# The head of a two-layer decoder trunk on one core: where its small loads are issued, how x is scaled, and in what order its first steps stand

## The chip, the core and the metric

The kernel runs on one core of one Trainium2 chip. The metric is device time in microseconds (us); the figure for a kernel is the median of its runs. Engines: TensorE (PE, its weight loads PEld), VectorE (DVE), ScalarE (ACT), GpSimd (POOL), and SyncE (SP), which issues most DMAs. The engines work side by side, each through its own list of instructions in a fixed order; they wait for one another on semaphores.

## What is computed

A hybrid decoder trunk over 256 tokens of width 1024: two layers, each of three parts (a half-step SwiGLU FFN, a mixer, another FFN). Every part begins with an RMS norm and a shift and a scale that come from a conditioning vector c. Only the start matters here:

```python
cond = jax.nn.silu(c)
mod = (cond @ ada_w[i] + ada_b[i]).reshape(B, N_SUB, 3, 1, D)
h = rms_norm(x, norm_g[i, 0]) * (1.0 + mod[:, 0, 1]) + mod[:, 0, 0]
x = x + 0.5 * mod[:, 0, 2] * swiglu(h, ffn_w_up[i, 0], ffn_w_down[i, 0])
```

Before any product of the first FFN can be made, two slices of `ada_w` (scale and shift) have to be loaded and multiplied by `cond`. All is float32; the kernel gets there by splitting each operand into a high part (float32r) and a low part, and by three matmuls for each product (high x high, high x low, low x high).

## The kernel before, in words

**The head.** The first FFN starts with seven of its 22 column blocks at once (`HEAD = 7`: three accumulators in the pool `mm`, four in the pool `aux`), and goes through the contraction in eight steps of 128 (q = 0 to 7). What a step needs, and the words used for it below:

- *chain q*: the 1 MB piece of `ada_w` for this step (two buffers), multiplied by `cond` on VectorE in eight instructions (lines 430 and 432, tile `adc`).
- *sums q*: eight small matmuls on TensorE that add the chain up over the partitions (line 444, tile `adac`), and then three tiny VectorE instructions (lines 450 and 453, tile `headmod`), which give shift and scale.
- *casts and low splits q*: the 0.9 MB weight piece (two buffers, a and b) is cast on ScalarE to its high part (line 356, `wh`), and VectorE subtracts it for the low part (line 357, `wl`).
- *shift q*: ScalarE makes `u` from the normed x (line 583) and its high part (line 586); VectorE makes the low part (line 587, *low h q*).
- *products q*: 42 matmuls (lines 726 to 728), seven blocks x two halves x three.

**The order.** Each load, cast, chain and so on is written into the program in a certain order, and a list scheduler then fixes each engine's order when the kernel is built: at each point it takes, of the instructions that it holds to be ready, the one written first. `issue_after(i)` adds that an instruction stands behind i on i's engine. In the loop of lines 577 to 592, step q writes chain q+1, then sums q and shift q, then products q-1; while products are written, each group of three calls `tick`, which writes one more piece of the next splits (`pump`, up to two weight pieces ahead). The VectorE part of sums q is put behind `last_chain`, the chain that was written last: chain q+1. So chain 1 stands ahead of sums 0.

**The loads.** All large loads go through SP's queue into eight buffers of 512 KB (`raw`), in the order in which they are used: chain 0, weights 0, chain 1, weights 1, and so on; a buffer is loaded again when its last reader is done. The two halves of x come before them. Six small loads (norm gains, `ada_b`, three more vectors, constants; lines 515 to 520) are issued in between, two behind each of the first three large ones (lines 524 to 528).

**The rest of the start.** ScalarE squares x; POOL makes the reciprocal root (line 556); TensorE transposes x and ScalarE copies it to `self.x` (line 614); VectorE scales x by the root (line 559, two instructions of 128x1024) and TensorE and ScalarE do the same for the scaled x (`xn`). Two groups of transposes (lines 561 and 566) turn the small rows into columns `vec` and `adab`, which the sums need.

**After the head** the other 15 blocks follow with 48 matmuls each, then the down projection, and then the five other parts; the products of these are spread with loads and splits in the same manner.

## Time and profile before

| | |
|---|---|
| median of 3 runs | 1098.29 us (1098.12 to 1099.98) |
| profiled execution | 1097.96 us, its span 1096.2 us |
| PE / DVE / ACT busy | 98% / 81% / 54% of the span |
| DMA | 260.26 MB, mean 237 GB/s, about 330 GB/s up to 150 us |
| first product of the head starts | 21.20 us |

How the rows are read: in a timeline a row is start (us), duration (us), engine, line, operation, output<-inputs, shapes, count, and in brackets the idle time of the engine before it with what ended it; several instructions of one kind in a row are one line. SPq and the like are the engine's sequencer, which issues DMAs. A window row gives, for a stretch of time, the busy time of each engine with its number of instructions, then TensorE's granted clock, the busy share of the DMA engines and GB/s.

### The profile page before, as it was taken

Reading aid. Unit: us, or ns where it says so; the run is one execution under the profiler, and the core shown is the slowest. Engines: PE = TensorE matmul, PEld = TensorE weight load, DVE = VectorE, ACT = ScalarE, POOL = GpSimd, SP = SyncE. Lnnn points to the kernel's source line nnn. Section 1 sums busy time; section 2 is a strip of 40 time slices with the busy share of each in tenths; the row PEclk is TensorE's granted clock in tenths of the full one; section 3 lists DMA queues with packets and bytes.
Section 4 is the critical chain, followed back from the end, with each engine's and each line's share of the span. In section 5 each row is a group of like instructions: output and inputs, shape, how many; then the busy total and the mean of one; then the engine's idle time right before and its main releaser. Section 6 shows DMA issues by size and latency. Waiting matters only on the chain.

```text
span 1096.2 us, 22151 instructions
## 1 busy us (share of the span) xinstructions
PE 1072.4 (98%) x8835; PEld 1049.2 (96%) x8835; DVE 883.3 (81%) x1598; ACT 586.7 (54%) x1105; POOL 23.1 (2%) x46
## 2 busy tenths in 40 slices
PE   6999999999999999999999999999999999999997
PEld 6999999988899999999999999999998999999997
DVE  6989999589895999888779999977987879555542
ACT  5364444486864754433555444445677756444443
POOL 0000000010000000000000000000000000000000
PEclk9999999999999999999999999999999999999999
DMA  9999999569774589999959999985653356665530
GB/s 299 335 332 331 329 322 320 169 211 352 243 248 117 154 272 329 298 285 303 263 173 274 320 329 350 313 241 173 192 154 116 117 164 191 185 190 176 177 113 39
DMA packets 304707, 260.26 MB, mean 237 GB/s; under 512 B 9524, under 2 KB 281500, under 8 KB 304604
## 3 DMA queue, kind: packets, MB, share of 16 engines
q1 hardware_dynamic: 304172, 257.80, 77.0%
q8 instruction: 69, 1.13, 0.4%
q0 software_dynamic: 288, 0.52, 0.2%
q10 hardware_dynamic: 144, 0.52, 0.1%
q14 instruction: 34, 0.28, 0.1%
HBM read 257.77 MB, written 1.05 MB: 236 GB/s over the span
## 4 chain that ended last, share of the span: by engine, by line
PE 62%; issue 19%; DVE 9%; DMA 5%; ACT 3%; POOL 1%; SPq 0%; POOLq 0%; DVEq 0%; ACTq 0%
PE pf L727 13%; PE pf L726 13%; PE pf L728 13%; PE pd L726 5%; PE pd L728 5%; PE pd L727 5%; DMA raw<-in_ada_w_dram 5%; DVE wl L368 3%; DVE adaacc L408 2%; ACT wh L367 1%; PE pA L1170 1%; PE pv L879 1%; PE pv L877 1%; PE pv L878 1%; PE sc L996 1%
## 5 line engine op out<-in xcount | busy, mean ns | idle before, releaser
L727 PE MATMUL pf<-hbuf,wh 128*128 128x256 f32 (+1 forms) x1920 | 542.0, 283 | 0.9 <-DVE hbuf L587 0.9
L728 PE MATMUL pf<-hbuf,wl 128*128 128x256 f32 (+1 forms) x1920 | 540.7, 283 | 0.0
L726 PE MATMUL pf<-hbuf,wh 128*128 128x256 f32 (+1 forms) x1920 | 537.8, 284 | 0.6 <-ACT hbuf L586 0.6
L367 ACT CAST wh<-raw 128x1024 fp32r<-128x1024 f32 x338 | 341.3, 1026 | 289.8 <-PE pf L727 158.3
L368 DVE TENSOR_TENSOR wl<-raw,wh 128x1024 fp32r<-128x1024 f32 x338 | 400.5, 1193 | 110.3 <-ACT wh L367 109.4
L727 PEld LDWEIGHTS pf<-hbuf,wh 128*128 128x128 f32 x1920 | 362.8, 189 | 2.2 <-DVE hbuf L587 1.6
L726 PEld LDWEIGHTS pf<-hbuf,wh 128*128 128x128 f32 x1920 | 361.8, 190 | 1.0 <-ACT hbuf L586 0.6
L728 PEld LDWEIGHTS pf<-hbuf,wl 128*128 128x128 f32 x1920 | 362.4, 189 | 0.2 <-issue 0.2
L728 PE MATMUL pd<-gx,wl 128*128 128x256 f32 x704 | 196.5, 279 | 1.1 <-DVE wl L368 1.1
L726 PE MATMUL pd<-gx,wh 128*128 128x256 f32 x704 | 197.2, 280 | 0.0
L727 PE MATMUL pd<-gx,wh 128*128 128x256 f32 x704 | 196.3, 279 | 0.0
L408 DVE SCALAR_TENSOR_TENSOR adaacc<-raw,cond,adaacc 128x1024 f32<-128x1024 f32 x112 | 143.4, 1280 | 17.5 <-DMA raw<-in_ada_w_dram 16.5
L728 PEld LDWEIGHTS pd<-gx,wl 128*128 128x128 f32 x704 | 132.6, 188 | 1.5 <-DVE wl L368 1.5
L726 PEld LDWEIGHTS pd<-gx,wh 128*128 128x128 f32 x704 | 133.4, 189 | 0.1
L727 PEld LDWEIGHTS pd<-gx,wh 128*128 128x128 f32 x704 | 132.3, 188 | 0.0
L792 ACT CAST gx<-g 128x256 fp32r<-128x256 f32 x88 | 35.6, 407 | 78.2 <-DVE g L834 70.9
L794 DVE TENSOR_TENSOR gx<-g,gx 128x256 fp32r<-128x256 f32 x88 | 36.7, 419 | 0.2
L834 DVE TENSOR_TENSOR g<-sa,pf 128x256 f32<-128x256 f32 x73 | 30.1, 414 | 0.3 <-ACT sa L833 0.2
L799 DVE SCALAR_TENSOR_TENSOR x<-pd,mod,x 128x256 f32<-128x256 f32 x32 | 14.3, 479 | 19.5 <-PE pd L728 19.5
L460 DVE STREAM_TRANSPOSE adatr<-adaacc 128x256 f32<-128x256 f32 x64 | 28.3, 442 | 1.4
L461 DVE TENSOR_REDUCE adared<-adatr 128x8 f32<-128x256 f32 x64 | 26.7, 418 | 1.6
L833 ACT ACTIVATE sa<-pf 128x256 f32<-128x256 f32 x73 | 27.4, 376 | 0.0
(219 smaller groups left out, 872.8 us busy)
## 6 DMA issues: line engine op xcount, KB each, us to landing
raw<-in_ffn_w_up_dram SPq DMA_DIRECT2D x162, 512.0 KB, 5.9
raw<-in_ada_w_dram SPq DMA_DIRECT2D x128, 512.0 KB, 6.0
raw<-in_ffn_w_down_dram SPq DMA_DIRECT2D x76, 512.0 KB, 5.5
raw<-in_fox_w_in_dram SPq DMA_DIRECT2D x32, 512.0 KB, 5.2
raw<-in_hgrn_w_in_dram SPq DMA_DIRECT2D x32, 512.0 KB, 4.1
raw<-in_ada_w_dram SPq DMA_DIRECT2D x32, 256.0 KB, 6.6
raw<-in_ffn_w_up_dram SPq DMA_DIRECT2D x16, 448.0 KB, 6.0
raw<-in_fox_w_out_dram SPq DMA_DIRECT2D x8, 512.0 KB, 4.6
```

Source lines behind the costliest of these rows:

```text
L367: nc.scalar.copy(wh[:, ks, cs], raw)
L368: nc.vector.tensor_tensor(wl[:, ks, cs], raw, wh[:, ks, cs].bitcast(F32), ALU.subtract)
L408: nc.vector.scalar_tensor_tensor(self.ada_acc, raw, self.cond[:, k:k + 1], self.ada_acc, ALU.mult, ALU.add)
L460: nc.vector.transpose(tr, total[:, o:o + S])
L461: nc.vector.tensor_reduce(red[:, o // 32:(o + S) // 32], tr.rearrange("p (b j) -> p b j", j=32), AX.X, ALU.add)
L726: nc.tensor.matmul(ps, wh, hx[:, :n], start=first, stop=False, skip_group_check=True)
L727: nc.tensor.matmul(ps, wh, hx[:, lo:lo + n], start=False, stop=False, skip_group_check=True)
L728: nc.tensor.matmul(ps, wl, hx[:, :n], start=False, stop=last, skip_group_check=True)
L792: nc.scalar.copy(dst[:, :S], v)
L794: nc.vector.tensor_tensor(dst[:, lo:lo + S], v, dst[:, :S].bitcast(F32), ALU.subtract)
L833: nc.scalar.activation(sa, ps[0], AF.Silu)
L834: nc.vector.tensor_tensor(g, sa, ps[1], ALU.mult)
```

## The change

It touches the head alone:

- The six small loads go to GpSimd's queue, ahead of the large loads in the program; SP issues only c, the identity, x and the large ones.
- x is copied to `self.x` by ScalarE and VectorE in turn (two copies each). x is scaled by ScalarE instead of VectorE, in pairs of 128 columns with their transposes and copy right behind each pair: eight instructions of 128x256 for two of 128x1024.
- The transposes for `vec` and `adab` share one PSUM bank.
- Shift 0 comes ahead of the loop. Sums 0 no longer stand behind chain 1, but behind the first low split of weights 0 (`first_low`). The casts of weights 1 stand behind the high part of h 0, and chain 1 behind low h 0.
- Products q are written in two pieces, blocks 0 to 2 (`HEAD_CUT = 3`) and blocks 3 to 6, and sums and shift q+1 stand between them. Written ahead of sums q+1 by the ticks of the first piece are, for q = 0, chain 1 and splits 1 (its second piece writes chain 2 and splits 2), and for q >= 1 chain q+2 and splits q+2: so `last_chain` of sums 2 is still chain 3, of sums 3 chain 4, and so on; sums 1 now stand behind chain 1.

```diff
@@ -1,5 +1,5 @@
 import math
-from contextlib import ExitStack
+from contextlib import ExitStack, nullcontext
 
 import numpy as np
 
@@ -38,7 +38,7 @@
 HEAD = 7
 QW = 128
 NPE = 0
-DEEP = 3
+HEAD_CUT = 3
 HG_LAG = (4, 3, 4, 10, 12)
 FOX_LAG = (24, 6)
 HG_ORDER = [("hgq", 0), ("hgv", 0), ("hgq", 1), ("hgq", 2), ("hgv", 1), ("hgq", 3),
@@ -353,8 +353,11 @@
                 for cs in cuts:
                     raw = self.take_raw()
                     raw = raw if HEAD > 4 else raw[:, 0, :]
-                    nc.scalar.copy(wh[:, k, cs], raw)
-                    nc.vector.tensor_tensor(wl[:, k, cs], raw, wh[:, k, cs].bitcast(F32), ALU.subtract)
+                    with self.tc.issue_after(self.last_shift[0]) if p[1] == 1 else nullcontext():
+                        nc.scalar.copy(wh[:, k, cs], raw)
+                    v = nc.vector.tensor_tensor(wl[:, k, cs], raw, wh[:, k, cs].bitcast(F32), ALU.subtract)
+                    if p[1] == 0 and cs.start == 0:
+                        self.first_low = v.ins
                     yield
             self.ready[i] = (kind, wh, wl)
             return
@@ -427,7 +430,8 @@
                                          start=first, stop=False, skip_group_check=True)
                         first = False
                 elif k < NPE + 2:
-                    nc.vector.tensor_scalar(ac[:, k % 2], raw[:, i, :], self.cond[:, k:k + 1], None, ALU.mult)
+                    with self.tc.issue_after(self.last_shift[1]) if q == 1 else nullcontext():
+                        nc.vector.tensor_scalar(ac[:, k % 2], raw[:, i, :], self.cond[:, k:k + 1], None, ALU.mult)
                 else:
                     v = nc.vector.scalar_tensor_tensor(ac[:, k % 2], raw[:, i, :], self.cond[:, k:k + 1],
                                                        ac[:, k % 2], ALU.mult, ALU.add)
@@ -446,7 +450,7 @@
         for part in (1, 0):
             b = l * 72 + (s * 3 + part) * 8 + q * n
             m = self.head_mod[:, part, q * n:(q + 1) * n]
-            with self.tc.issue_after(self.last_chain):
+            with self.tc.issue_after(self.last_chain if q else self.first_low):
                 nc.vector.tensor_tensor(m, ps[:, part * n:(part + 1) * n], self.adab[:, b:b + n], ALU.add)
             if part == 1:
                 g = (l * 3 + s) * 8 + q * n
@@ -520,12 +524,10 @@
                  (cst, a["consts"][:, P:])]
         for dst, src in small[:2]:
             nc.sync.dma_start(dst, src)
-        small = small[2:]
+        for dst, src in small[2:]:
+            nc.gpsimd.dma_start(dst, src)
         while len(self.raw_queue) < RAW_BUFS:
             self.emit_raw()
-            for dst, src in small[:2]:
-                nc.sync.dma_start(dst, src)
-            small = small[2:]
         self.ones = cp.tile([P, P], F32, name="ones")
         nc.vector.memset(self.ones, 1.0)
         self.selq = cst[:, 128:144]
@@ -554,28 +556,30 @@
             nc.scalar.activation(xs[t], xt[t], AF.Square, accum_out=ms[:, t:t + 1])
         nc.vector.tensor_scalar(ms, ms, 1.0 / D, EPS, ALU.mult, ALU.add)
         self.last_pow = nc.gpsimd.tensor_tensor(ms, ms, self.mhalf, ALU.pow).ins
-        self.load_x(xt, self.x)
-        for t in range(2):
-            nc.vector.tensor_scalar(xs[t], xt[t], ms[:, t:t + 1], None, ALU.mult)
+        self.load_x(xt, self.x, engines=(nc.scalar.copy, nc.vector.tensor_copy))
+        self.vec = cp.tile([P, 80], F32, name="vec")
+        self.adab = cp.tile([P, 144], F32, name="adab")
+        self.head_mod = cp.tile([P, 2, KC], F32, name="headmod")
         pr = self.bank("pr")
-        nc.tensor.transpose(pr[:, :80], rows, self.ident[:80, :80])
-        self.vec = cp.tile([P, 80], F32, name="vec")
+        nc.tensor.transpose(pr[:, 0:80], rows, self.ident[:80, :80])
+        for l in range(2):
+            nc.tensor.transpose(pr[:, P + l * 72:P + (l + 1) * 72], abr[:, l, :], self.ident[:72, :72])
         nc.vector.tensor_copy(self.vec, pr[:, :80])
-        pa = self.bank("pa")
-        for l in range(2):
-            nc.tensor.transpose(pa[:, l * 72:(l + 1) * 72], abr[:, l, :], self.ident[:72, :72])
-        self.adab = cp.tile([P, 144], F32, name="adab")
-        nc.vector.tensor_copy(self.adab, pa[:, :144])
-        self.head_mod = cp.tile([P, 2, KC], F32, name="headmod")
-
-        self.load_x(xs, xn)
+        nc.vector.tensor_copy(self.adab, pr[:, P:P + 144])
+        for k in range(0, KC, 2):
+            for t in range(2):
+                c = slice(k * P, (k + 2) * P)
+                nc.scalar.activation(xs[t][:, c], xt[t][:, c], AF.Copy, scale=ms[:, t:t + 1])
+            self.load_x(xs, xn, k, k + 2)
         self.pf = [self.acc("pf") for _ in range(3)] + [self.bank("pf") for _ in range(HEAD - 3)]
         self.pf = [self.halves(p) for p in self.pf]
         l, s = divmod(self.subs[0], NSUB)
         n = QW // P
-        cur = []
-        for q in range(D // QW):
-            while self.n_split < min(2 * q + DEEP, 2 * D // QW):
+
+        def shift(q):
+            while self.n_split < min(2 * q + 1, 2 * D // QW):
+                self.split_step()
+            if q == 0:
                 self.split_step()
             self.head_mods(l, s, q)
             for k in range(q * n, (q + 1) * n):
@@ -586,12 +590,15 @@
                 v0 = nc.scalar.copy(h[:, :S], u)
                 v1 = nc.vector.tensor_tensor(h[:, HS:HS + S], u, h[:, :S].bitcast(F32), ALU.subtract)
                 self.last_shift = (v0.ins, v1.ins)
-            for t in cur:
-                self.head_products(*t)
+        shift(0)
+        for q in range(D // QW):
             wh, wl = self.weights("upk")
-            cur = [(q * n + i, wh[:, i], wl[:, i]) for i in range(n)]
-        for t in cur:
-            self.head_products(*t)
+            for i in range(n):
+                self.head_products(q * n + i, wh[:, i], wl[:, i], 0, HEAD_CUT)
+            if q + 1 < D // QW:
+                shift(q + 1)
+            for i in range(n):
+                self.head_products(q * n + i, wh[:, i], wl[:, i], HEAD_CUT, HEAD)
         with self.tc.issue_after(self.last_pow):
             for o in (0, 64):
                 nc.gpsimd.memset(self.bf[o:o + 64, :], 0.0)
@@ -604,17 +611,18 @@
             nc.vector.tensor_copy(self.identb, self.ident)
             nc.vector.tensor_copy(self.maskb, cst[:, 0:P])
 
-    def load_x(self, src, dst):
-        nc = self.nc
-        for k in range(0, KC, 2):
+    def load_x(self, src, dst, k0=0, k1=KC, engines=None):
+        nc = self.nc
+        engines = engines or (nc.scalar.copy,)
+        for k in range(k0, k1, 2):
             px = self.bank("px")
             for i in range(4):
                 nc.tensor.transpose(px[:, i * P:(i + 1) * P], src[i % 2][:, (k + i // 2) * P:(k + i // 2 + 1) * P],
                                     self.ident)
-            nc.scalar.copy(dst[:, k:k + 2, :].rearrange("p k c -> p (k c)"), px)
-
-    def head_products(self, k, wh, wl):
-        for b in range(HEAD):
+            engines[k // 2 % len(engines)](dst[:, k:k + 2, :].rearrange("p k c -> p (k c)"), px)
+
+    def head_products(self, k, wh, wl, b0, b1):
+        for b in range(b0, b1):
             for c in range(2):
                 o = (c * HEAD + b) * P
                 self.mm3(self.pf[b][c], wh[:, o:o + P], wl[:, o:o + P], self.hbuf[0][:, k, :],
```

## The prediction

> **What bounds the kernel now.** First the page:
>
> ```profile
> span 1096.2 us, 22151 instructions
> PE 1072.4 (98%) x8835; PEld 1049.2 (96%) x8835; DVE 883.3 (81%) x1598; ACT 586.7 (54%) x1105; POOL 23.1 (2%) x46
> ```
>
> TensorE is busy for all but 23.8 us of the span. Most of that lies ahead of the first product, so the change can win only where it acts: in the head, 21 of 1096 us before the first product and some 49 us of products. Windows next, because a bound differs from stage to stage, and the waits of 20 to 220 us:
>
> ```profile
> 0.00:21.00 21.00, 11.53 (x52) 10.56 (x52) 11.53 (x30) 12.62 (x21) 2.39 (x11) 1.00 0.98 290
> 52.00:58.00 6.00, 6.00 (x52) 5.84 (x51) 5.61 (x14) 2.59 (x5) 0.00 (x0) 1.00 1.12 338
> 100.00:120.00 20.00, 20.00 (x175) 19.84 (x174) 18.10 (x23) 9.12 (x14) 0.00 (x0) 1.00 1.14 332
> ```
>
> ```profile
> ACT wh L367 <- PE pf L727: 32.3, 12, 3.2
> ACT wh L356 <- DMA raw<-in_ffn_w_up_dram: 17.9, 6, 4.2
> ```
>
> In the first 21 us no compute engine is full (11.53, 11.53 and 12.62 us), but the DMA is (0.98). In the head's turns everything is full at once: TensorE 6.00 of 6, VectorE 5.61 of 6, DMA 1.12 at 338 GB/s. The two waits separate the stages. Casts of the head (L356) wait for their data to land; casts behind the head (L367) wait for TensorE to give a buffer back, so behind the head the supply is ahead and TensorE alone sets the pace. A shift of the head's end should therefore reach the end of the kernel in full, and one that is made up inside the head should not be seen at all. What counts is when products 7 start.
>
> The chain into the first product, from the timelines:
>
> ```profile
> 7.89 0.69 POOL L556 TENSOR_TENSOR rstd<-rstd,mhalf 128x2 f32<-128x2 f32 x1 [7.03 <-DVE rstd L555]
> 11.66 0.94 ACT L356 CAST wh<-raw 128x896 fp32r<-128x896 f32 x1 [1.81 <-DMA raw<-in_ffn_w_up_dram]
> 12.10 0.37 PE L561 MATMUL pr<-ident,startbig 80*128 80x80 f32 x1 [2.87 <-DMA cst<-in_consts_dram]
> 13.04 1.07 DVE L357 TENSOR_TENSOR wl<-raw,wh 128x896 fp32r<-128x896 f32 x1
> 18.96 0.22 DVE L450 TENSOR_TENSOR headmod<-adac,adab 128x1 f32<-128x1 f32 x2
> 19.41 0.60 ACT L583 ACTIVATE u<-startbig,headmod 128x256 f32<-128x256 f32 x1 [0.39 <-DVE headmod L453]
> 20.74 0.40 ACT L586 CAST hbuf<-u 128x256 fp32r<-128x256 f32 x1
> 21.20 1.86 PE L726 MATMUL pf<-hbuf,wh 128*128 128x256 f32 x7 [0.56 <-ACT hbuf L586]
> ```
>
> Sums 0 run at 18.96, behind chain 1, though the low split that they are now put behind was over at 14.11. Then shift 0, then products 0 at 21.20. VectorE's turn and TensorE's turn in the running head:
>
> ```profile
> 31.21 0.21 DVE L450 TENSOR_TENSOR headmod<-adac,adab 128x1 f32<-128x1 f32 x2
> ...
> 35.12 0.61 DVE L430 TENSOR_SCALAR adc<-raw,cond 128x256 f32<-128x256 f32 x2
> ...
> 38.03 0.21 DVE L450 TENSOR_TENSOR headmod<-adac,adab 128x1 f32<-128x1 f32 x2
> ...
> 38.29 1.09 DVE L357 TENSOR_TENSOR wl<-raw,wh 128x896 fp32r<-128x896 f32 x1
> 39.87 1.09 DVE L357 TENSOR_TENSOR wl<-raw,wh 128x896 fp32r<-128x896 f32 x1 [0.49 <-ACT wh L356]
> 40.88 0.42 DVE L587 TENSOR_TENSOR hbuf<-u,hbuf 128x256 fp32r<-128x256 f32 x1
> 41.22 0.61 DVE L430 TENSOR_SCALAR adc<-raw,cond 128x256 f32<-128x256 f32 x2
> ```
>
> ```profile
> 27.70 0.79 PE adac L444 x8
> ...
> 33.56 0.79 PE adac L444 x8
> 34.34 0.93 PE pf L726 x7
> ...
> 39.70 0.79 PE adac L444 x8
> 40.49 0.93 PE pf L726 x7
> ...
> 57.95 0.80 PE adac L444 x8
> ```
>
> From start to start VectorE takes 2.91 for a chain, 0.26 for sums, 1.01 for a low split (39.87 to 40.88), 0.34 for low h: 2.91 + 0.26 + 2 x 1.01 + 0.34 = 5.53, and with the 0.49 that it waits for a cast and small gaps its turn is 6.10 (35.12 to 41.22). TensorE's own turn is 5.86 (27.70 to 33.56, where it waits for nothing); then it is 6.14, and (57.95 - 39.70) / 3 = 6.08. So VectorE, by a hair, sets the turn.
>
> **The change, part by part.**
>
> *Small loads to POOL.* The rows' transposes waited for these loads until 12.10. POOL is idle from 0.85 to 7.89; six issues at 0.56 each (the one below) end by 4.3, and the landing that the same queue shows, 6.1 from its issue, puts the last at about 9.8, before 12.10 and long before sums 0 need them. POOL's root at 7.89 isn't held up. Worth of it for the path: nothing; the bounds are 0.6 later (0.2 MB shared with x at 290 GB/s, were x to wait for all of it) and 0 earlier, as sums 0 are later than both.
>
> ```profile
> 62.65 0.56 POOL L601 DMA_DIRECT2D tm<-in_tmat_dram  x1 [52.48 <-DVE lmask L600]
> tm<-in_tmat_dram POOLq DMA_DIRECT2D x1, 64.0 KB, 6.1
> L652 ACT ACTIVATE hbuf<-x,gs x40: 492/502/512, 173.0 to 898.3; 128x256 fp32r<-128x256 f32 x40
> L614 ACT COPY startbig<-px x4: 585/588/599, 13.6 to 16.2; 128x512 f32<-128x512 f32 x4
> ```
>
> The window's DMA share of 0.98 at 290 GB/s says that a second queue finds no idle engine. [...] Were the queues separate, chain and weight loads would land 0.2 MB / 290 GB/s = 0.7 earlier, and the sum below would be lower by that.
>
> *First product.* From the root's end at 8.6, ScalarE has a copy left to 9.0, then eight scalings (0.50 each, the L652 row, the nearest with a scale column) and four copies (0.59). As its instructions overlap by some 0.1, that is 8 x 0.40 + 4 x 0.49 = 5.2; the last copy waits about 0.3 for its four transposes. Cast a of weights 0, written later, has landed at 11.66 but comes behind: 14.5 to 15.4. Low split to 16.5, sums to 16.9, u to 17.5, high h to 17.9: products 0 at about 18.0 instead of 21.20. If the scheduler takes the cast at its landing, as before, the low split ends at 14.1 and products start at 15.6; if cast b falls on the path too, 19.0. I take 18.0: all scalings are written first and are ready.
>
> *VectorE behind it.* Chain 1 ran beside the start; now it stands behind low h 0, at 18.4, and until then VectorE has, beyond chain 0, only two low splits, sums 0 and a few copies to do. That is the price. From 18.4: chain 1, two low splits, sums 1, chain 2, low h 1, two low splits, chain 3: 3 x 2.91 + 4 x 1.01 + 0.26 + 0.34 = 13.4, so chain 3 ends at 31.8, while sums 2 that stand behind it ran at 31.21 before. Products 1 gain some 3 us; products 2 gain nothing. They follow sums by 2.5 (38.03 to 40.49) to 3.1 (31.21 to 34.34): 34.3 to 34.9 if sums come first, against 34.34.
>
> *The order of sums and low splits.* Low splits q+2 are now written ahead of sums q+1. If the scheduler holds cast a to be done when the chain ends, one low split goes first, +1.0; if both, +2.0 and more, because then sums wait for the landing of buffer b. The trace has this choice once, at the end of the head:
>
> ```profile
> 56.31 0.22 DVE L450 TENSOR_TENSOR headmod<-adac,adab 128x1 f32<-128x1 f32 x2
> ...
> 56.58 1.09 DVE L357 TENSOR_TENSOR wl<-raw,wh 128x896 fp32r<-128x896 f32 x1
> 58.77 0.22 DVE L450 TENSOR_TENSOR headmod<-adac,adab 128x1 f32<-128x1 f32 x2 [1.10 <-PE adac L444]
> ...
> 60.05 0.42 DVE L587 TENSOR_TENSOR hbuf<-u,hbuf 128x256 fp32r<-128x256 f32 x1
> ```
>
> ```profile
> 60.53 0.39 PE L727 MATMUL pf<-hbuf,wh 128*128 128x256 f32 x1 [0.86 <-DVE hbuf L587]
> ```
>
> ```profile
> 48.84 0.94 ACT L356 CAST wh<-raw 128x896 fp32r<-128x896 f32 x1 [2.60 <-DMA raw<-in_ffn_w_up_dram]
> ...
> 54.63 0.94 ACT L356 CAST wh<-raw 128x896 fp32r<-128x896 f32 x1 [2.29 <-DMA raw<-in_ffn_w_up_dram]
> ...
> 64.88 1.05 ACT L367 CAST wh<-raw 128x1024 fp32r<-128x1024 f32 x1 [2.92 <-PE pf L727]
> ```
>
> Sums 7 (58.77) were written behind both low splits 7 and still slipped in between them, as cast b was not held to be done. So I expect sums directly behind the chain or behind one low split.
>
> *The end of the head is pinned.* Chain 7 and weights 7 come by a DMA that is full from start to end; weights 7a landed at 54.63, chain 7's last piece lies just ahead of it in the queue. 448 KB at 338 GB/s are 1.4, so that piece lands at about 53.3, and four of the chain's eight instructions (2.91 / 8 each) are still to run, 1.5: sums 6 at 54.8 at best, 1.5 before the old 56.31, or, behind low split 7a (54.63 + 0.94 + 1.05), at 56.6. Products 6 (57.95 + 0.80 = 58.75 before) then start between 57.3 and 59.1, whatever happened earlier.
>
> *What is gained there.* Sums 7 stood on TensorE between products 5 and 6 and on VectorE ahead of low h 6: hence the idle 0.86 at 60.53. Now sums 7 are in the middle of products 6. From 58.75 to products 6's end at 64.88 it took 6.13; now 5.86 for the whole turn, sums included: -0.3.
>
> *Sum.* Sums directly behind the chain at the old 56.31: 0 - 0.3 = -0.3 (with the best landing -1.8). Behind one low split: +0.3 - 0.3 = 0. The likeliest is -0.3: from 1097.96 to 1097.7 for the profiled execution (its span 1096.2 and 1.8 around it), which lies 0.33 below the median of the runs; so **1098.0** for the median. About 0.2% (2.2 us) is what a measurement tells from no change; this is no change.
>
> **Rivals.**
>
> *The early start goes through.* Products 0 at 15.6 give VectorE 2.4 us more than in my sum: chain 3 is then at its landing, and turns go at TensorE's 5.86 instead of 6.08. From products 1 on nothing waits, and of the 5.6 us at the start the 3.2 of my own sum pass through: 1095.1. For it: the cast was taken at its landing at 11.66, and VectorE's turn is 5.53 without gaps. Against it: the DMA at 1.12 pins chain 7, which leaves -1.8 at best unless loads also land earlier. Chance of a gain above 2.2: 0.20.
>
> *Slower: low splits first.* If both low splits stand ahead of sums, sums 6 wait for weights 7b, which follow 7a by some 1.2 (448 KB at 338 GB/s is 1.4): 54.63 + 1.3 + 0.94 + 1.09 = 58.0 instead of 56.31, +1.7, less 0.3: +1.4, 1099.7. It decides from the first turn in which VectorE is later than cast a, and then stays, as it is the written order. For it: my chain 3 ends at 31.8, near to the landing of weights 3. TensorE would stand from products 1's end (18.0, then 27.70 - 21.20 + 0.79 = 7.3, then 5.86: 31.2) to about 37. Its first seven products cost 1.86 at 21.20 but 0.93 at 34.34: standing so long it may be slow again, +0.9 for those seven alone: 1100.6. [...] Chance 0.25, half of it above +2.2.
>
> *Nothing but a shuffle.* Products 0 start no earlier than 19, or the scheduler keeps the old order: within 0.5 of before. This is in "same".
>
> **How the numbers follow.** My case with the shuffle 0.55 (1096.6 to 1098.8), going through 0.20 (1095.1 to 1096.5), low splits first 0.25 (1099 to 1100.9). The range 8 in 10 leaves out the ends of both: 1095.3 to 1100.6. Faster by over 0.2%: 0.22, as earlier landings in my own case could also reach it; slower: 0.15; same 0.63.
>
> **What would show it.** Right: products 0 near 18, TensorE standing 3 us or more between products 1 and 2, products 2 within 1.5 of 34.3, casts of the head still released by DMA, the idle 0.86 gone, products 6 ending at 63.5 to 65. Wrong: products 2 at 31 to 32 with no gap (supply wasn't the bound), or a gap of 6 us and slow products behind it.

## The result and the profile after

The changed kernel takes 1104.8 us (median of 6 runs, 1103.2 to 1106.0) against 1098.07 us for the kernel before (median of 6, 1097.75 to 1099.98): a ratio of 1.0060, with a 95% interval of 1.0049 to 1.0071. It is 6.7 us slower; the forecast was 1098.0, and the range ended at 1100.6. The profiled execution took 1105.38 us.

The page of the changed kernel, busy times:

```profile
span 1103.6 us, 22163 instructions
...
PE 1075.6 (97%) x8835; PEld 1051.9 (95%) x8835; DVE 882.4 (80%) x1598; ACT 590.6 (54%) x1111; POOL 26.7 (2%) x52
```

The span is 7.4 us longer, and TensorE is busy only 3.2 us longer (1072.4 before): 4.2 us are idle time, and 3.2 us more go into the same instructions, which run longer at a lower clock (mean granted clock of the profiled execution 0.993, 0.998 before). Nearly all of the 7.4 lies in the head, whose end moves by 6.98. First its start, from the timelines of TensorE, VectorE, GpSimd and ScalarE (start, duration, engine, line, what is written from what, count, idle time before and what ended it):

```profile
5.78 1.12 PE L620 MATMUL px<-ident,startbig 128*128 128x128 f32 x4 [2.39 <-DMA startbig<-in_x_dram]
...
8.11 0.19 ACT L556 ACTIVATION_READ_ACCUMULATOR startbig<-startbig 128x1 f32 x1
...
9.60 0.36 PE L564 MATMUL pr<-ident,startbig 80*128 80x80 f32 x1 [2.70 <-DMA startbig<-in_final_norm_g_dram]
...
10.00 2.76 PE L620 MATMUL px<-ident,startbig 128*128 128x128 f32 x12
...
10.24 0.24 DVE L567 COPY vec<-pr 128x80 f32<-128x80 f32 x1 [9.24 <-PE pr L566]
...
12.13 0.16 DVE L557 TENSOR_SCALAR rstd<-rstd 128x2 f32<-128x2 f32 x1
...
12.44 0.72 POOL L558 TENSOR_TENSOR rstd<-rstd,mhalf 128x2 f32<-128x2 f32 x1 [7.47 <-DVE rstd L557]
```

The root's arguments were there at 8.30, when ScalarE had its squares (the row at 8.11). But the root runs at 12.44, and at 7.89 before. The transposes of the small rows (L564) now stand behind the first 4 of x's 16 transposes, not behind all of them; they wait for the last small row to land until 9.60, and the other 12 of x wait behind them. On VectorE the copy of the rows (L567), the next two small steps and a copy of x all stand ahead of the root's step (L557). Two engines, each in its fixed order, hold up a step that needs neither the small rows nor the transposed x.

A smaller part of the delay isn't order. In the kernel before, ScalarE's squares end 0.76 earlier, at 7.54:

```profile
7.35 0.19 ACT L554 ACTIVATION_READ_ACCUMULATOR startbig<-startbig 128x1 f32 x1
```

ScalarE and TensorE waited there for x until 5.1, in the changed kernel until 5.8. This goes with the queue: with the small loads on GpSimd's queue ScalarE's timelines have the squares end at 8.02 (root_first), 8.17 (before_pool), 8.30 (the changed kernel), 8.40 (late_root) and 8.54 (order_pool), with them on SyncE's queue at 7.54 (the kernel before), 7.57 (order_sync) and 7.95 (small_sp).

Then the running head, timelines of VectorE, TensorE and ScalarE:

```profile
23.22 0.61 DVE L434 TENSOR_SCALAR adc<-raw,cond 128x256 f32<-128x256 f32 x2
...
36.47 2.08 DVE L358 TENSOR_TENSOR wl<-raw,wh 128x896 fp32r<-128x896 f32 x2
38.47 0.21 DVE L454 TENSOR_TENSOR headmod<-adac,adab 128x1 f32<-128x1 f32 x2
38.74 1.36 PE L448 MATMUL adac<-ones,adc 128*128 128x1 f32 x8 [2.11 <-DVE headmod L454]
...
40.38 0.40 ACT L590 CAST hbuf<-u 128x256 fp32r<-128x256 f32 x1
...
40.84 1.86 PE L734 MATMUL pf<-hbuf,wh 128*128 128x256 f32 x7 [0.74 <-ACT hbuf L590]
```

Chain 1 starts at 23.22, behind low h 0, and VectorE works without a pause until chain 3 ends at 36.5. Then both low splits of weights 3 (36.47) go ahead of sums 2 (38.47), and products 2 start at 40.84 instead of 34.21. Products 1 had ended at 36.63. The windows of the changed kernel (busy time and instructions of TensorE, its loads, VectorE, ScalarE and GpSimd; then the granted clock, DMA share, GB/s) show what that pause does:

```profile
34.00:40.00 6.00, 3.89 (x30) 3.69 (x29) 6.00 (x17) 2.00 (x4) 0.00 (x0) 0.94 1.12 333
40.00:46.00 6.00, 5.26 (x25) 5.18 (x26) 6.00 (x17) 2.63 (x5) 0.00 (x0) 0.50 1.14 335
46.00:52.00 6.00, 6.00 (x52) 6.00 (x52) 4.09 (x11) 1.79 (x2) 0.00 (x0) 0.99 1.14 334
```

VectorE is full through both windows (6.00 of 6). TensorE's granted clock reads 0.50 from 40 on, until 46.2 (0.92 in the microsecond from 46): 25 instructions fit into 5.26 us of work, where 52 fit into 6.00 behind it.

The table holds, from the traces, the start of the root's step on VectorE, of products 0, 1 and 2, how long products 2 took (6.0 with sums 3 among them, 5.2 to 5.5 without, at the full rate: granted clock 1.00 from 34 to 40 in the kernel before), and the start of the first block behind the head. The last column is the time against the kernel before, run beside it.

| kernel | root's step | products 0 | 1 | 2 | length of 2 | block | ratio to before (95%) |
|---|---|---|---|---|---|---|---|
| before | 7.57 | 21.20 | 28.35 | 34.21 | 5.5 | 69.84 | 1 |
| changed | 12.13 | 22.83 | 30.06 | 40.84 | 7.6 | 76.82 | 1.0060 (1.0049 to 1.0071) |
| root_first | 8.05 | 17.74 | 26.93 | 38.16 | 6.6 | 73.12 | 1.0033 (1.0017 to 1.0050) |
| small_sp | 9.01 | 18.66 | 26.27 | 34.52 | 7.1 | 71.20 | 1.0006 (0.9996 to 1.0015) |
| sums_first | 12.69 | 23.08 | 30.66 | 39.15 | 6.8 | 74.29 | 1.0032 (1.0017 to 1.0048) |
| warm | 12.65 | 23.35 | 31.82 | 42.17 | 6.0 | 76.61 | 1.0056 (1.0038 to 1.0075) |
| before_pool | 10.88 | 22.31 | 30.07 | 35.92 | 5.2 | 70.77 | 1.0013 (1.0004 to 1.0022) |
| order_sync | 8.62 | 19.88 | 29.07 | 34.94 | 6.0 | 72.52 | 1.0011 (1.0002 to 1.0019) |
| order_pool | 8.57 | 19.44 | 27.22 | 33.10 | 6.0 | 67.86 | 0.9967 (0.9955 to 0.9979) |
| order_pool_warm | 8.02 | 18.64 | 25.60 | 31.58 | 6.0 | 66.31 | 0.9965 (0.9952 to 0.9978) |
| late_root | 12.09 | 22.48 | 30.45 | 36.33 | 6.0 | 71.10 | 0.9996 (0.9987 to 1.0005) |
| no_pin | 8.03 | 18.64 | 26.96 | 33.62 | 6.1 | 68.77 | 0.9980 (0.9970 to 0.9989) |
| order_sync_even | 7.78 | 19.46 | 27.84 | 33.72 | 6.0 | 68.18 | 0.9960 (0.9946 to 0.9975) |
| after_fill | 12.09 | 22.79 | 29.76 | 40.71 | 6.0 | 75.14 | 1.0039 (1.0027 to 1.0052) |

The block's start moves by +6.98 between the first two rows. From products 0 to it: +1.63 at products 0, +0.08 more at products 1, +4.92 more at products 2 (6.63 in all), then +1.3 more at products 3 (48.28, 40.35 before, 7.93 in all: the clock costs some 2.2 in products 2, and sums 3 no longer stand behind them), and -0.95 in the five turns behind.

### The profile page after: what moved, and what is told of

Same layout as the page of the kernel before. It is cut to its first block, busy times and chain, and to the rows that moved or that the text cites. A ratio compares the mean times of both kernels' runs of the same rounds, so it can differ in the third digit from the quotient of the medians.

```text
span 1103.6 us, 22163 instructions
## 1 busy us (share of the span) xinstructions
PE 1075.6 (97%) x8835; PEld 1051.9 (95%) x8835; DVE 882.4 (80%) x1598; ACT 590.6 (54%) x1111; POOL 26.7 (2%) x52
## 4 chain that ended last, share of the span: by engine, by line
PE 73%; issue 18%; ACT 3%; DVE 3%; POOL 1%; DMA 1%; POOLq 0%; DVEq 0%; ACTq 0%
PE pf L734 16%; PE pf L735 16%; PE pf L736 16%; PE pd L734 6%; PE pd L735 5%; PE pd L736 5%; ACT wh L370 1%; PE pA L1178 1%; PE pv L887 1%; PE pv L885 1%; PE pv L886 1%; PE sc L1004 1%; DVE wl L358 1%; PE pt L1026 1%; DMA startbig<-in_final_norm_g_dram 1%
```

## The experiments

The theory from the two traces: two faults of order, one at the start and one behind it, and the clock behind a pause on top. The rivals: the loads on GpSimd's queue cost by themselves; the DMA pins the head's end, so that no order helps; the half clock comes from something other than the pause.

**root_first.** Only the order at the start, by hand:

```diff
-        nc.vector.tensor_scalar(ms, ms, 1.0 / D, EPS, ALU.mult, ALU.add)
+        self.ms_step = nc.vector.tensor_scalar(ms, ms, 1.0 / D, EPS, ALU.mult, ALU.add).ins
...
+        with self.tc.issue_after(self.ms_step):
+            self.load_x(xt, self.x, engines=(nc.scalar.copy, nc.vector.tensor_copy))
...
+        with self.tc.issue_after(self.last_px):
+            nc.tensor.transpose(pr[:, 0:80], rows, self.ident[:80, :80])
...
+        with self.tc.issue_after(self.ms_step):
+            nc.vector.tensor_copy(self.vec, pr[:, :80])
```

(Not shown are the lines that these replace, the same wait for the copy of adab, and where `last_px` is set: it is the last transpose of x.)

> The changed kernel, with one difference: VectorE's copies of the small rows and of x stand behind the step in front of the root, and TensorE's transposes of the small rows stand behind those of x. The loads stay on GpSimd's queue. My theory (the order at the start costs the early start, and what is late there is handed on in full): the root ends at about 9.1 instead of 13.16, products 0 start at 19.0 instead of 22.83, chain 1 and all that is queued behind it comes 3.8 earlier, products 2 at 37.0 instead of 40.84, with the idle stretch and the slow clock still in front of and in them; the whole is 3.8 us shorter than the changed kernel. Rival A (the loads on GpSimd's queue themselves take the time, by sharing the DMA with x and the chains): the root comes at most 0.6 earlier, the whole is within 1 us of the changed kernel. Rival B (the DMA sets when products 2 can start): products 0 start early, products 2 stay near 40.8, the whole within 1 us of the changed kernel.

Measured: 1100.91 us, 3.9 below the changed kernel (3.0 by the two ratios). Products 0 start at 17.74, near the 18.0 of the prediction's own sum. The rest of its head, from the timelines of ScalarE, TensorE and VectorE:

```profile
17.74 1.01 PE L738 MATMUL pf<-hbuf,wh 128*128 128x256 f32 x3 [2.64 <-ACT hbuf L593]
...
23.81 0.94 ACT L357 CAST wh<-raw 128x896 fp32r<-128x896 f32 x1 [3.77 <-DMA raw<-in_ffn_w_up_dram]
...
25.84 0.60 ACT L590 ACTIVATE u<-startbig,headmod 128x256 f32<-128x256 f32 x1
...
26.93 0.75 PE L738 MATMUL pf<-hbuf,wh 128*128 128x256 f32 x4 [1.75 <-ACT hbuf L593]
...
32.55 2.09 DVE L358 TENSOR_TENSOR wl<-raw,wh 128x896 fp32r<-128x896 f32 x2
34.56 0.22 DVE L454 TENSOR_TENSOR headmod<-adac,adab 128x1 f32<-128x1 f32 x2
...
36.87 0.94 ACT L357 CAST wh<-raw 128x896 fp32r<-128x896 f32 x1 [1.13 <-DMA raw<-in_ffn_w_up_dram]
...
38.16 1.86 PE L738 MATMUL pf<-hbuf,wh 128*128 128x256 f32 x7 [2.28 <-ACT hbuf L593]
```

The theory holds in size, and a fault shows that it did not have: sums 1 were over at 23.5, but u 1 (25.84) stands on ScalarE behind the casts of weights 2, the first of which waits until 23.81 for its load. The same stands ahead of products 2: the high part of h 2 comes behind a cast of weights 4, which waits until 36.87 for its load. Low splits 3 are ahead of sums 2 here too.

**small_sp.** The small loads back on SyncE's queue, in the loop that issues the first weight loads:

```diff
-        for dst, src in small[2:]:
-            nc.gpsimd.dma_start(dst, src)
+        small = small[2:]
         while len(self.raw_queue) < RAW_BUFS:
             self.emit_raw()
+            for dst, src in small[:2]:
+                nc.sync.dma_start(dst, src)
+            small = small[2:]
```

> The changed kernel with the small loads back on SyncE's queue, between the first weight loads as before; all else as changed. The scheduler then sets the small rows' transposes behind those of x by itself. My theory (order): the root ends near 8.6 to 9.1 and products 0 start at 18 to 19.2, the whole 3.5 to 4.8 us shorter than the changed kernel, the same as with the order alone mended within 0.8. Rival A (the loads on GpSimd's queue take the time by themselves): this one is at least 2 us shorter than the kernel with only the order mended. Rival B (the DMA pins products 2): within 1 us of the changed kernel.

Measured: 1098.67 us, 6.1 below the changed kernel and 2.2 below root_first. That passes the bound set for rival A. But the trace doesn't point to the loads: products 0 start 0.9 later than in root_first. What differs lies behind, in VectorE's and TensorE's timelines:

```profile
32.35 0.22 DVE L454 TENSOR_TENSOR headmod<-adac,adab 128x1 f32<-128x1 f32 x2
...
32.62 1.09 DVE L358 TENSOR_TENSOR wl<-raw,wh 128x896 fp32r<-128x896 f32 x1
...
34.52 1.09 PE L736 MATMUL pf<-hbuf,wh 128*128 128x256 f32 x7 [0.84 <-ACT hbuf L592]
```

Here sums 2 come ahead of the low splits, and products 2 start at 34.52, inside the 34.3 to 34.9 that the prediction gave for that order. One source, another queue for six loads, and the order on three engines is different. Whether the queue or the order makes the 2.2 was open until order_sync_even.

**sums_first.** Low splits q+2 written behind sums q+1 from q = 1 on:

```diff
+            cut = HEAD_CUT if q == 0 else 1
             for i in range(n):
-                self.head_products(q * n + i, wh[:, i], wl[:, i], 0, HEAD_CUT)
+                self.head_products(q * n + i, wh[:, i], wl[:, i], 0, cut)
```

(The second piece starts at `cut` in the same way.)

> The changed kernel, with the first piece of products 1 and later cut to one block, so that the low splits of weights q+2 are written behind sums q+1 from q = 1 on: sums 2 then stand directly behind chain 3 on VectorE. The first turn is as in the changed kernel, the late root too. My theory (the two low splits ahead of sums 2 hold products 2 up by 2.0, and the idle stretch on TensorE that this gives costs 2.3 more by a halved clock): sums 2 at 36.5 instead of 38.47, products 2 at about 38.8 instead of 40.84, the idle stretch before them under 2.5 us, no half clock in products 2, the whole 4.3 us shorter than the changed kernel. Rival A (half clock has another cause than the idle stretch): products 2 still 2 us earlier but as slow, the whole 2.0 shorter. Rival B (the order doesn't matter, products 2 wait for what the DMA brings): no change, within 0.7.

Measured: 1101.03 us, 3.8 below the changed kernel (3.1 by the two ratios, expected 4.3). Products 2 start 1.7 earlier though products 0 start 0.25 later. The profiled execution, one of the longer ones (1103.13), has a half clock in products 2 all the same (granted clock 0.50 in the microseconds from 41 and 42), behind 1.2 us of idle time on TensorE (from 36 to 40, in windows of 1 us; 2.9 in the changed kernel from 36 to products 2 at 40.84). So the half clock doesn't need a pause as long as the changed kernel's.

**warm.** 16 matmuls behind products 1, into columns that nothing reads:

```diff
+            if q == 1:
+                for i in range(16):
+                    nc.tensor.matmul(self.spare2[:, 256:512], wh[:, 0, 0:P], self.hbuf[0][:, 1, :S],
+                                     start=False, stop=False, skip_group_check=True)
```

> The changed kernel with 16 matmuls of 128x256 added behind products 1 on TensorE, into columns of a bank that nothing reads; more work, and nothing else. They wait, as sums 3 did, for VectorE's sums 2, so they run from about 38.6 on, and sums 3 move into products 2. My theory (products 2 ran at half rate because TensorE had stood idle for some 3.4 us or more, with only eight tiny matmuls in it): the idle stretch is now 2 us, the added matmuls run at the full rate (0.12 each) and end at 40.6, products 2 start at 40.8 to 41.0 as before but take 5.9 instead of 7.6, and the whole is 1.5 to 1.8 us shorter than the changed kernel in spite of the added work. Rival (the half rate comes with a start after any wait, or with what stands on the other engines just then): the added matmuls run at 0.21 each, end at 42, and the whole is 0.5 to 1.3 us longer.

Measured: 1104.55 us, not to be told from the changed kernel. The profile shows in that place what was expected: from the end of products 1 to the block behind the head 38.5 us, 40.2 in the changed kernel, 1.7 less. But products 0 ran 8.6 us instead of 7.4, at about half the rate until 29: the microseconds from 27 and from 28 hold 7 and 5 matmuls, the next one 11, though the granted clock of all three reads 1.00. Time was gained at one place and lost at another; after_fill repeats it with both places filled.

**before_pool.** The kernel before, with its loop for the small loads replaced by the two lines that small_sp takes out.

> The kernel before with one edit of the change alone: the six small loads are issued on GpSimd's queue. My theory (the edit turns the scheduler's order at the start, and that is what costs): as in the changed kernel, TensorE's transposes of the small rows now stand behind the first four of x and wait for the last of these loads, and VectorE's copies of the rows stand ahead of the step in front of the root, so the root ends at about 13 instead of 8.58; on VectorE the two scalings of x come behind most of chain 0, products 0 start at 23.5 to 25 instead of 21.20, and nothing makes it good: the whole is 2.5 to 3.8 us longer than before, 1100.7 to 1102. Rival (the order at the start is free, there is slack up to products 0, or the loss in the changed kernel comes from the other edits): within 1 us of before.

Measured: 1098.84 us against 1097.92, ratio 1.0013. Timelines of TensorE, VectorE and GpSimd:

```profile
9.42 0.37 PE L559 MATMUL pr<-ident,startbig 80*128 80x80 f32 x1 [2.61 <-DMA startbig<-in_final_norm_g_dram]
...
10.88 0.16 DVE L553 TENSOR_SCALAR rstd<-rstd 128x2 f32<-128x2 f32 x1
11.19 0.72 POOL L554 TENSOR_TENSOR rstd<-rstd,mhalf 128x2 f32<-128x2 f32 x1 [6.21 <-DVE rstd L553]
```

So the queue alone turns the order, in the kernel before too: the root is 3.3 late. But it costs 0.9 to 1.4 us here, not the 2.5 to 3.8 expected. In this kernel sums 0 stand behind chain 1 on VectorE as well, and they come only 1.1 later (20.07 instead of 18.96): the root had some slack. The change took that wait away, and with it the slack.

**order_sync.** small_sp, and sums behind their own chain, with the splits one weight ahead in the head:

```diff
-        last = self.main[min(self.mpos + SPLIT_AHEAD, len(self.main) - 1)]
+        last = self.main[min(self.mpos + self.ahead, len(self.main) - 1)]
...
-            with self.tc.issue_after(self.last_chain if q else self.first_low):
+            with self.tc.issue_after(chain if q else self.first_low):
```

> The changed kernel with the small loads on SyncE's queue as before, and a second difference: sums q stand on VectorE behind their own chain q instead of behind the last chain written, and the splits run one weight ahead of TensorE in the head instead of two, so that sums 2 come ahead of chain 3 (and behind both low splits 2). My theory (what was left of the loss with the loads on SyncE's queue is VectorE's backlog: chain 3 ahead of sums 2 and the idle and slow TensorE it gives): sums 2 at about 29.6 instead of 32.35, products 2 directly behind products 1 at 32.3 instead of 34.52, no half clock behind them, turns of 5.9, the block behind the head at 67.5 instead of 71.20; the whole about 3.5 us shorter than with the loads on SyncE's queue alone, 1095, some 3 us below before. Rival (the DMA sets the end of the head): weights 3 to 7 land no earlier, the block behind the head starts at 69 to 70 and the whole is within 1 us of before.

Measured: 1099.13 us; the theory failed. Products 1 and 2 follow each other directly (29.07, 34.94), but from products 4 on the turns are 6.84. VectorE's timeline:

```profile
44.43 0.23 DVE L454 TENSOR_TENSOR headmod<-adac,adab 128x1 f32<-128x1 f32 x2 [1.10 <-PE adac L448]
...
44.57 1.08 DVE L359 TENSOR_TENSOR wl<-raw,wh 128x896 fp32r<-128x896 f32 x1
...
51.28 0.23 DVE L454 TENSOR_TENSOR headmod<-adac,adab 128x1 f32<-128x1 f32 x2 [1.13 <-PE adac L448]
```

Sums now stand on VectorE ahead of the low splits, and wait 1.1 us a turn for TensorE's sums, which stand amid the products. Sums too early cost too: from products 4 to the block it takes 25.7 us, in order_sync_even 22.7. The DMA of the rival it was not: between 40 and 70 us no wait for a load is listed.

**order_pool.** The loads on GpSimd's queue, the start of root_first, the two lines of order_sync, and the casts behind the shift:

```diff
-                    with self.tc.issue_after(self.last_shift[0]) if p[1] == 1 else nullcontext():
+                    with self.tc.issue_after(self.last_shift[0]) if p[1] >= 1 else nullcontext():
```

(In what was expected, the run beside it is order_sync.)

> The changed kernel with the small loads on GpSimd's queue as changed, and the order made as in the run beside it by hand: small rows behind x on TensorE and behind the root's step on VectorE, sums behind their own chain, splits one weight ahead, and ScalarE's casts of weights q+1 behind shift q, so that shift 1 no longer waits behind casts 2. My theory (it is the order that costs, not the queue): products 0 at 17.7, products 1 directly behind them at 25.3, products 2 at 31.3, the block behind the head at 66.6, the whole 0.5 to 1.2 us shorter than the same order with the loads on SyncE's queue, about 1094.3. Rival A (loads on GpSimd's queue cost by themselves): at least 1 us longer than with the loads on SyncE's queue. Rival B (the DMA sets the end of the head): the same as the run beside it, both within 1 us of before.

Measured: 1093.64 us (1092.95 to 1096.77) against 1097.92: ratio 0.9967, 3.6 (by the ratio) to 4.3 below before and 10.2 to 11.2 below the changed kernel. ScalarE's, VectorE's and TensorE's timelines:

```profile
25.55 0.60 ACT L590 ACTIVATE u<-startbig,headmod 128x256 f32<-128x256 f32 x1 [4.48 <-DVE headmod L457]
...
28.41 2.08 DVE L359 TENSOR_TENSOR wl<-raw,wh 128x896 fp32r<-128x896 f32 x2
30.82 0.23 DVE L454 TENSOR_TENSOR headmod<-adac,adab 128x1 f32<-128x1 f32 x2 [0.33 <-PE adac L448]
...
33.10 0.98 PE L739 MATMUL pf<-hbuf,wh 128*128 128x256 f32 x7
```

Products follow each other without idle time from 19.44 to the head's end, in turns of 5.9 from products 1 on, and the block starts 2.0 before that of the kernel before. The small loads, the scalings on ScalarE, chain 1 behind low h 0 and the sums amid the products are all still in it: none of them, by itself, makes the kernel slow.

**order_pool_warm.** The same with 12 matmuls of the cast weights with themselves, between sums 0 and products 0.

(The run beside it is order_pool.)

> The run beside it with 12 matmuls of 128x256 added on TensorE between sums 0 and products 0, of the cast weights with themselves, into a bank that products 0 then overwrite; more work and nothing else. They fill the 2.6 us in which TensorE waits for shift 0. Theory of the clock (its rate is set by how full the stretch of some 3.4 us before was, and the first products of every kernel so far ran at half rate because TensorE stood idle ahead of them): the first products take 0.12 instead of 0.21 each, products 0 take about 5.9 instead of 7.4, everything behind starts 1.0 to 1.6 earlier, the whole is 1.0 to 1.6 us shorter than the run beside it, if VectorE keeps up. Rival (half rate at the start has another cause, such as the time since the program began): products 0 as slow as before, and the whole the same within 0.4.

Measured: 1093.53 us, not to be told from order_pool. Products 0 took 7.1 in the profiled execution, against 7.9. The sign is right, the size half of what was expected, and the runs spread by 4 us; in time this is inconclusive.

**late_root.** order_pool, with the start left as changed (none of the lines of root_first).

(The run that beat both kernels is order_pool, here and in the next two.)

> The run that beat both kernels, with one part of its order taken back: at the start the small rows stand where the changed kernel has them, ahead of x on TensorE and ahead of the root's step on VectorE. Behind the start the three engines have the order of that run. My theory (the late root is one cause, worth its 3.5 to 4.5, and the order behind the start another, worth some 7): root at about 13, products 0 at 22.8 as in the changed kernel, products 1 and 2 directly behind each other with no idle stretch, the block behind the head at about 71.3, the whole 3.4 to 4.3 us longer than the run that beat both, 1097.5, and so some 7 us shorter than the changed kernel. Rival A (the late root is harmless once the order behind it is right): within 1.5 us of the run that beat both. Rival B (the late root is the cause of nearly all): over 5 us longer than it.

Measured: 1097.79 us, ratio 0.9996; the block starts 3.24 later than in order_pool. As expected, and both rivals fall. With root_first it closes a square:

| ratio to before | start as changed | start by hand |
|---|---|---|
| order behind it as changed | 1.0060 | 1.0033 |
| order behind it by hand | 0.9996 | 0.9967 |

The start is worth 0.27% or 0.29% (3.0 to 3.2 us), the order behind it 0.64% or 0.66% (7.0 to 7.2 us), each the same, within the intervals, whatever the other is.

**no_pin.** order_pool without its line on the casts.

> The run that beat both kernels, with one part taken back: ScalarE's casts of weights 2 no longer stand behind shift 1, and so ahead of it, where they wait for weights 2 to land. My theory (part of what was left with only the start mended is shift 1 behind casts 2): products 1 start 1.5 to 2 us later than at the end of products 0, with some 1.7 more where a half-clock stretch follows; the whole 1.6 to 3.3 us longer than the run that beat both, 1095.2 to 1097. Rival (VectorE sets products 1 and 2 whatever ScalarE does): within 0.7 us of it.

Measured: 1097.07 us, ratio 0.9980: by ratios 1.4 us above order_pool, by medians 3.4, with intervals that overlap, so the times alone don't exclude the rival. The profiled execution is the fastest of its nine (1094.5). In it products 0 start 0.8 earlier than in order_pool and the block 0.9 later, so that 1.7 is lost in between. The sign is as expected; the size is held to no better than 1 to 3 us.

**order_sync_even.** order_pool's order with the loads on SyncE's queue and sums behind both low splits:

```diff
-            with self.tc.issue_after(chain if q else self.first_low):
+            with self.tc.issue_after(self.last_low if q else self.first_low):
```

> The order of the run that beat both kernels with the small loads on SyncE's queue, as before; this time sums 1 to 7 are also put behind both low splits, so that VectorE's turn is the same as there. Only the queue of the six loads differs, and what it turns at the start (the rows' copies behind the first low split, scalings in one row). My theory (the queue costs and gives little; the earlier run with the loads on SyncE's queue was slow because its sums stood in front of the low splits and VectorE waited for TensorE's): the turns are 5.9 to 6.0, products 0 at 18.5 to 19, the whole 0 to 1.2 us longer than with the loads on GpSimd's queue. Rival (the queue matters by itself): a difference of over 2 us, in either direction.

Measured: 1094.0 us, ratio 0.9960 (0.9946 to 0.9975), within the interval of order_pool. With the order made by hand, the queue itself shows no effect on the time, though the intervals don't exclude one of 2 us. At the start it shows: the root's step, which the squares release in both, starts at 7.78 here, at 8.57 in order_pool. The prediction read from the window's DMA share (0.98 at 290 GB/s) that a second queue finds no idle engine. This pair of runs agrees: 1094.0 us here, 1093.64 with the second queue.

**after_fill.** The changed kernel with warm's 16 matmuls and order_pool_warm's, here 11, in its two pauses.

> The changed kernel with matmuls of 128x256 added in its two idle stretches on TensorE, 11 between sums 0 and products 0 and 16 between products 1 and 2; more work, none of it used. Theory of the clock (the rate goes down after a stretch of some 3.4 us that was less than about half full, and up after one that was full): products 0 take 6 to 7 instead of 7.4, which helps nothing, since products 2 wait for VectorE; products 2 take 6 instead of 7.6 and the whole is 1.2 to 1.8 us shorter than the changed kernel, about 1103.2. Rival (no link between the filling and the rate): products 2 as slow as before, the whole 0 to 1 us longer than the changed kernel.

Measured: 1103.13 us, 1.7 below the changed kernel (2.3 by the two ratios) in spite of 27 matmuls more. TensorE's timelines, first a row of the changed kernel, then this one's:

```profile
42.49 0.41 PE L735 MATMUL pf<-hbuf,wh 128*128 128x256 f32 x1
...
38.71 2.16 PE L610 MATMUL adac<-hbuf,wh 128*128 128x256 f32 x16 [2.10 <-DVE headmod L457]
40.71 0.40 PE L744 MATMUL pf<-hbuf,wh 128*128 128x256 f32 x2
40.94 0.28 PE L745 MATMUL pf<-hbuf,wh 128*128 128x256 f32 x1
```

Products 2 start where they did (40.71), but one matmul takes 0.28 instead of 0.41 (granted clock 1.00 from 40 to 43, 0.50 in the changed kernel), and the block behind the head starts 1.68 earlier. In the profiled executions of both runs that fill this pause, warm and this one, products 2 take 6.0 instead of 7.6. So the half clock there does come from the pause.

## Why the prediction was wrong

*First product: the step failed.* Its sum came out (18.0; 17.74 with the start mended, though the root ended there at 9.1), its first line was wrong: "from the root's end at 8.6". The small loads were put down as worth "nothing" because they would land by 9.8, long before sums 0 need them. They did land so (9.60). What was missed is that in the source TensorE's transposes of the rows, and VectorE's copies of them, are free to move past x; only GpSimd's queue was looked at for what could be held up. The root came 4.5 late, products 0 at 22.83. Of the 4.5, 0.76 is x itself: the bound of "0.6 later" that was set aside (0.2 MB / 290 GB/s is 0.7), and the rest is order.

*VectorE behind it: right.* 13.4 us from chain 1's start to chain 3's end; measured 23.22 to 36.5. It named VectorE as what sets products 2.

*The order of sums and low splits: the wrong one was taken.* The rival "low splits first", at 0.25, is what came, in the changed kernel (36.47, then 38.47) and in root_first. The one case of the trace of before from which the choice was argued, sums slipping between two low splits at 58.77, showed a cast that came late. In the changed kernel both casts of weights 3 were over at 35.3, ahead of chain 3's end at 36.5. The late start wasn't needed for it: in root_first chain 3 ends at 32.6, behind cast a (over at 32.0) and ahead of cast b (33.2), and the low splits go first all the same. The rival's own words, "from the first turn in which VectorE is later than cast a", hold in both.

*The clock: a term too small.* The rival put 0.9 on the first seven products. Products 2 took 7.6, at a granted clock of 0.50 until 46.2, where 5.2 to 5.5 is the full rate: some 2.2. With the pause filled, 1.7 came back although sums 3 (0.8) then stood among products 2.

*The head's end is pinned by the DMA: the step that made the sum 0, and it failed too.* Products 6 were to start between 57.3 and 59.1, "whatever happened earlier", so that lateness would be made up inside the head. In the changed kernel they start at 65.94: what was late at products 2 stayed late. Nor did the pin bound from below: in order_pool they start at 56.67, and none of the waits listed from 20 us on is a cast of the head waiting for its load.

*Turns of 5.86 at the end: right.* The idle 0.86 is gone, and products 4 to 7 come every 5.86 on average (54.20 to 71.78 for three). That gave back 0.95 in five turns; 0.3 was forecast for the one of products 6.

*A side reading.* Of TensorE's 23.8 idle us, 9.5 lie ahead of the first product (21.00 less 11.53), not most of them.

Together: with the start and the order behind it made by hand the change is worth 3.6 us (order_pool); the late start takes 3.0 to 3.2 and the order behind it 7.0 to 7.2, which together make the 6.7 us by which the changed kernel is slower.

What stays open: how the 7 us of the order behind the start divide between sums behind their own chain, splits one weight ahead and the casts behind the shift. Only the casts were taken back alone, and in sums_first the low splits alone were moved, for 3.1 to 3.8. Freeing chain 1 from its place behind low h 0 wasn't tried. Why the scheduler turned the order is argued, not shown: a load moved to another queue has another expected landing there.

## What to carry to other kernels

Where a scheduler orders each engine's instructions, moving a load to another queue is also an edit to the order on every engine that reads it: list what may now pass what, and pin the steps on the path by hand. Taking a wait off a path makes what stood behind its slack count: here a root 3.3 later cost the kernel before 0.9 to 1.4 us, and one 3.5 to 4.1 earlier gave the changed order 3.0 to 3.2 back. Ask of a consumer that shares an engine with the producer's next work which of the two is ahead once that engine is late, since that is when the written order decides.

## What the runs showed of the hardware

In root_first's profile the changes of TensorE's granted clock lie 3.42 or 6.82 us apart. Windows of 1 us, TensorE's busy time and its granted clock, then DMA share and GB/s:

```profile
24.00:25.00 1.00, 1.00 (x11) 1.00 1.09 326
25.00:26.00 1.00, 0.18 (x2) 1.00 1.27 299
26.00:27.00 1.00, 0.07 (x1) 1.00 1.16 285
27.00:28.00 1.00, 1.00 (x8) 0.76 1.24 326
28.00:29.00 1.00, 1.00 (x6) 0.50 1.02 384
29.00:30.00 1.00, 1.00 (x6) 0.50 1.00 388
30.00:31.00 1.00, 1.00 (x7) 0.53 1.14 323
31.00:32.00 1.00, 1.00 (x11) 1.00 1.21 294
...
37.00:38.00 1.00, 0.00 (x0) 0.88 1.20 300
...
41.00:42.00 1.00, 1.00 (x10) 0.91 1.01 377
```

Read as a step between 1.00 and 0.50, 0.76 over one microsecond means half rate from 27.52, 0.53 until 30.94; the second stretch runs from 37.76 (0.88) to 41.18 (0.91). The distances are 3.42, 6.82 and 3.42. By the same reading half rate lasts from 36.24 to 39.66 in small_sp and from 40.36 to 43.78 in sums_first, 3.42 us each, and from 39.32 to 46.16 in the changed kernel, 6.84.

The pause before the first stretch was only 1.75 us (products 0 end at 25.18, products 1 start at 26.93): of the 3.42 us up to 27.52 products filled 1.67 us, 49%, and the next 3.42 ran at half rate while TensorE was full (6 or 7 matmuls in a microsecond of 1.00 busy, 11 behind them). In small_sp products filled 1.72 of the 3.42 us up to 36.24 (products 2 start at 34.52), 50%, and half rate followed. In the changed kernel they filled 0.73 of the 3.42 us up to 39.32 (products 1 end at 36.63), 21%, and half rate followed; of the next 3.42 us they filled 1.90 at half rate (from 40.84), 56%, and half rate went on. What a pause costs wasn't set by its length alone in these profiles. That may be why runs of one kernel spread by 3 us and more, but it was not shown.

One pause far behind the head has the same length in two profiles and not the same cost. It lasts 1.20 us in the changed kernel (from 229.03) and 1.19 in the kernel before (from 222.06). Windows of 4 us behind it, the changed kernel first:

```profile
230.00:234.00 4.00, 3.77 (x18) 0.57 0.17 66
...
223.00:227.00 4.00, 3.75 (x31) 1.00 0.13 49
```

Half rate follows in the one execution (0.57) and not in the other (1.00), for the same work; by windows of 1 us it lasts from 230.5 to 233.9 in the changed kernel. That is up to 1.7 us (an estimate: half of these 3.4), so a part of the 3.2 us by which TensorE is busy longer in the changed kernel's profile comes from there and not from the head.
